# Sums of w_out's quarters made by GpSimd instead of VectorE, in a hybrid decoder layer

## The chip, the cores and the metric

The kernel runs on one core of a Trainium2 chip. What counts is the time of one execution on the device, in microseconds (us). TensorE does the matmuls, VectorE (DVE in the profile), ScalarE (ACT) and GpSimd (POOL) the elementwise work, and SyncE (SP) issues most of the DMAs; SPq is its queue.

## What is computed

One layer over 1024 positions of width 2048. The input is normalised and projected; one half of the projected columns goes through gated DeltaNet attention (group A), the other through a spatial gate in chunks of 128 positions (group B). The two results stand side by side, 2048 wide, and go through the output projection, a residual add and a last norm:

```python
def reference(x, norm_w, w_in, ..., w_out, final_norm_w):
    xn = rms_norm(h, norm_w[l])
    proj = xn @ w_in[l].astype(x.dtype)
    ...
    o_b = u_b * chunked_causal_sgu(v_n, w_spatial[l], b_spatial[l]) * jax.nn.silu(z_b)
    mix = jnp.concatenate([o_a, o_b], axis=-1) @ w_out[l].astype(x.dtype)
    h = h + mix
    return rms_norm(h, final_norm_w)
```

The change touches w_out alone, a 2048 x 2048 matrix in float32.

## The kernel before

The positions are worked in two halves of 512. Each half first does group A, then group B; after both comes one output phase. A matmul in float32 is made of three in a shorter format: each operand is split into a high part (a cast by ScalarE, L136) and a low part (what is left, a subtraction by VectorE, L137), and the three products hi x hi, hi x lo and lo x hi are added in PSUM (L238, L239, L241).

The output projection is done with seven block products instead of eight (Winograd's form of Strassen's scheme). For this the blocks of w_out are needed in four sums, T1 to T4. They are made ahead of time, while group B of each half runs, by the generator `w_sums` (L830): for each of eight k it loads four tiles of 128 x 512, one from each quarter of w_out (L837, tiles `ws{cb}_{k}_{i}`), adds and subtracts in place in a chain of four operations (L839, L840, L842, L843), and stores the four results to a buffer in DRAM, `wc_d` (L846). Half 0 makes the sums of one column block, half 1 those of the other. In the first of the four operations tile 0 takes tile 1 off, in the second tile 1 takes tile 2 off, in the third tile 2 adds tile 0, in the fourth tile 3 takes tile 2 off. So the third needs the first, and the fourth the third.

Tiles 0 and 1 share the buffers with the tag `o`, two of them; tiles 2 and 3 those with the tag `gae`, three. The quarters of the next k can thus be loaded into tiles 0 and 1 only when the stores of this k have landed. Such a round of loads, sums and stores is called a turn here.

At the same time TensorE multiplies the projection's weights. They come in chunks of 128 x 512 (`wr`, loaded at L187 by `w_chunk`), with three buffers for the raw chunk and four for each of its parts `wh` and `wl`. TensorE works twelve matmuls on a chunk. `wr_38_2` is chunk 2 of column tile 38. The list `tasks` holds generators, which `tick` moves on between matmuls; how far they run is told in ticks (`W_SUM0` = 84 ticks before the first turn; then 5, 1, 1 and 3 in a turn). The order on each engine is that of a scheduler, which goes by its own estimates of the durations, within what dependencies allow. Each engine works its list in order, and a DMA that has to wait at the head of SP's queue keeps back all that stand behind it.

Of the kernel before, what the change touches and what calls it, by code (L numbers as in the profile page):

```python
# [12 lines left out]
ALU = mybir.AluOpType  # L13
# [18 lines left out]
def kernel(ctx, tc, x_tok, x_t, w_in, w_v0, w_vb, w_out, conv_w, norm_w, a_log, dt_bias,  # L32
                       hn_w, sgu_w, sgu_b, wsp_t, b_sp, fn_w, out):
    nc = tc.nc
# [739 lines left out]
    def group_b(hf, xs, st):  # L774

        env, sb = {}, {}
        spawn(w_sums([(hf, k) for k in range(HK)]))
        for blk in range(1, 4):
            for k2 in range(KT // 2):
# [46 lines left out]
    def w_quarter(b, cb, k):  # L826

        return w_out[b[1] * 2 + cb, b[0] * HK + k]

    def w_sums(ck):  # L830

        yield W_SUM0
        for cb, k in ck:
            q = {}
            for i, b in enumerate(((1, 1), (0, 1), (0, 0), (1, 0))):
                q[b] = wk.tile([P, 1, T], F32, tag=("o", "gae")[i // 2], bufs=(2, 3)[i // 2], name=f"ws{cb}_{k}_{i}")
                nc.sync.dma_start(q[b], w_quarter(b, cb, k))  # L837
            yield 5
            nc.vector.tensor_tensor(q[1, 1], q[1, 1], q[0, 1], op=ALU.subtract)  # L839
            nc.vector.tensor_tensor(q[0, 1], q[0, 1], q[0, 0], op=ALU.subtract)  # L840
            yield 1
            nc.vector.tensor_tensor(q[0, 0], q[0, 0], q[1, 1], op=ALU.add)  # L842
            nc.vector.tensor_tensor(q[1, 0], q[1, 0], q[0, 0], op=ALU.subtract)  # L843
            yield 1
            for i, b in enumerate(((0, 1), (0, 0), (1, 1), (1, 0))):
                nc.sync.dma_start(wc_d[i, cb, k], q[b].rearrange("p o c -> p (o c)"))  # L846
            yield 3
# [238 lines left out]
```

## Time and profile before

| | us |
|---|---|
| median of 3 runs | 1749.18 (1749.1 to 1756.64) |
| the profiled execution | 1754.24 |
| its span in the trace | 1752.5 |

| engine | busy us | share of the span |
|---|---|---|
| TensorE, matmuls | 1724.6 | 98% |
| VectorE | 1222.7 | 70% |
| ScalarE | 823.5 | 47% |
| GpSimd | 95.3 | 5% |

The busy time is told of the span. Matmuls overlap, so a share of 98% says that TensorE hardly ever stood, not that it went at its peak. TensorE's clock has two levels; the granted clock is told as a share of the upper one. "Idle before" is the time that an engine stood before an instruction, and the name behind the arrow is what released it. The time of a DMA runs from its issue on the queue to its landing.

### The profile page before, as it was taken

The numbers are of one execution on the slowest core, as the hardware profiler recorded it, in microseconds if no ns is written. First come the engines' busy times: TensorE is split into PE (matmuls) and PEld (weight loads), VectorE is DVE, ScalarE is ACT, GpSimd is POOL, SyncE is SP. The second block draws the span as 40 slices with busy tenths as digits, with TensorE's granted clock in tenths as the row PEclk, the third lists the DMA queues.
The fourth block names the chain that finished last, engine by engine and source line by source line (L and its number), as shares of the span: only waits on it lengthen the run. The fifth ranks groups of instructions, "written<-read, shape, count | busy, mean of one in ns | idle before, by whom it ended". The sixth has DMA issues, their size and how long they took to land.

```text
span 1752.5 us, 27530 instructions
## 1 busy us (share of the span) xinstructions
PE 1724.6 (98%) x9334; PEld 1457.0 (83%) x9334; DVE 1222.7 (70%) x3015; ACT 823.5 (47%) x1952; POOL 95.3 (5%) x172
## 2 busy tenths in 40 slices
PE   9999999999999999999999999999999999999997
PEld 8878888888998887887888888899888788888886
DVE  7678697887836654757979789793665544766776
ACT  7573545546434322638555464642432234433454
POOL 1000010010100000000001001010010000000000
PEclk9999999999999999999999999999999999999999
DMA  7454445364533687426553645443268866666565
GB/s 251 107 144 128 115 119 151 97 177 127 133 101 106 198 287 246 131 63 172 138 136 93 169 106 150 136 130 106 67 174 275 263 195 204 214 186 192 160 196 200
DMA packets 190046, 277.99 MB, mean 159 GB/s; under 512 B 38064, under 2 KB 70864, under 8 KB 189648
## 3 DMA queue, kind: packets, MB, share of 16 engines
q1 hardware_dynamic: 185216, 263.60, 51.2%
q0 software_dynamic: 4544, 12.62, 2.9%
q8 instruction: 73, 1.20, 0.3%
q14 instruction: 69, 0.57, 0.1%
q10 hardware_dynamic: 144, 0.01, 0.0%
HBM read 220.54 MB, written 55.61 MB: 158 GB/s over the span
## 4 chain that ended last, share of the span: by engine, by line
PE 78%; DMA 9%; DVE 8%; issue 2%; ACT 2%; SPq 1%; POOL 0%; DVEq 0%; ACTq 0%; POOLq 0%
PE oa L1008 15%; PE acc L238 14%; PE acc L241 14%; PE acc L239 14%; PE vb L794 8%; DMA wr<-w_in 2%; DMA ws<-w_out 2%; DMA wc_d<-ws 2%; PE ds L637 1%; DVE wl L137 1%; PE p L626 1%; DVE cv L416 1%; PE first L307 1%; PE first L306 1%; PE first L308 1%
## 5 line engine op out<-in xcount | busy, mean ns | idle before, releaser
L238 PE MATMUL acc<-xh,wh 128*128 128x512 f32 x1472 | 593.1, 403 | 1.1 <-ACT wh L136 1.1
L241 PE MATMUL acc<-xh,wl 128*128 128x512 f32 x1472 | 579.5, 394 | 11.5 <-DVE wl L137 11.5
L239 PE MATMUL acc<-xl,wh 128*128 128x512 f32 x1472 | 577.2, 392 | 0.0
L136 ACT CAST wh<-wr 128x512 fp32r<-128x512 f32 x368 | 226.5, 617 | 421.2 <-PE acc L239 205.4
L241 PEld LDWEIGHTS acc<-xh,wl 128*128 128x128 f32 x1472 | 278.2, 189 | 73.4 <-DVE wl L137 15.2
L238 PEld LDWEIGHTS acc<-xh,wh 128*128 128x128 f32 x1472 | 278.8, 189 | 58.1 <-issue 3.4
L239 PEld LDWEIGHTS acc<-xl,wh 128*128 128x128 f32 x1472 | 278.6, 189 | 51.8 <-issue 0.2
L137 DVE TENSOR_TENSOR wl<-wr,wh 128x512 fp32r<-128x512 f32 x368 | 250.3, 684 | 96.3 <-ACT wh L136 93.4
L1008 PE MATMUL oa<-who,a 128*128 128x512 f32 x864 | 266.9, 389 | 0.0
L1008 PEld LDWEIGHTS oa<-who,a 128*128 128x128 f32 x864 | 162.3, 188 | 33.6
L1008 PE MATMUL oa<-wlo,a 128*128 128x512 f32 x432 | 168.2, 389 | 0.0
L416 DVE SCALAR_TENSOR_TENSOR cv<-pc,cw,cv 128x511 f32<-128x511 f32 (+1 forms) x144 | 107.1, 744 | 7.5 <-ACT cv L413 5.7
L794 PE MATMUL vb<-whvb,xh 128*128 128x256 f32 x384 | 110.6, 288 | 0.0
L136 ACT CAST who<-wro 128x512 fp32r<-128x512 f32 x108 | 66.7, 618 | 92.7 <-PE oa L1008 71.6
L137 DVE TENSOR_TENSOR wlo<-wro,who 128x512 fp32r<-128x512 f32 x108 | 73.9, 687 | 50.0 <-ACT who L136 49.4
L794 PE MATMUL vb<-whvb,xl 128*128 128x256 f32 x384 | 108.7, 283 | 0.0
L794 PE MATMUL vb<-wlvb,xh 128*128 128x256 f32 x384 | 108.7, 283 | 0.0
L1008 PEld LDWEIGHTS oa<-wlo,a 128*128 128x128 f32 x432 | 81.1, 188 | 16.8
L571 DVE TENSOR_TENSOR fst<-fs 32x31 f32<-32x31 f32 (+15 forms) x248 | 81.0, 327 | 4.4
L573 DVE TENSOR_TENSOR fs<-fs,fst 32x31 f32<-32x31 f32 (+15 forms) x248 | 81.0, 327 | 4.2
L794 PEld LDWEIGHTS vb<-whvb,xh 128*128 128x128 f32 x384 | 73.7, 192 | 0.2
L794 PEld LDWEIGHTS vb<-wlvb,xh 128*128 128x128 f32 x384 | 73.7, 192 | 0.0
(245 smaller groups left out, 2245.5 us busy)
## 6 DMA issues: line engine op xcount, KB each, us to landing
wr<-w_in SPq DMA_DIRECT2D x368, 256.0 KB, 3.4
ws<-w_out SPq DMA_DIRECT2D x64, 256.0 KB, 4.8
wc_d<-ws SPq DMA_DIRECT2D x64, 256.0 KB, 3.3
wro<-wc_d SPq DMA_DIRECT2D x64, 256.0 KB, 2.8
ar<-mix_d SPq DMA_DIRECT2D x56, 256.0 KB, 3.4
wrvb<-w_vb SPq DMA_DIRECT2D x48, 256.0 KB, 2.7
wro<-w_out SPq DMA_DIRECT2D x48, 256.0 KB, 2.7
xr<-x_t SPq DMA_DIRECT2D x32, 256.0 KB, 4.1
```

The lines of the kernel that those rows point to most:

```text
L136: nc.scalar.copy(hi, src)
L137: nc.vector.tensor_tensor(lo, src, hi.bitcast(F32), op=ALU.subtract)
L238: nc.tensor.matmul(acc, hi[:, kk, :], xh, start=(k == 0), stop=False)
L239: nc.tensor.matmul(acc, hi[:, kk, :], xl, start=False, stop=(last and lo is None))
L241: nc.tensor.matmul(acc, lo[:, kk, :], xh, start=False, stop=last)
L306: nc.tensor.matmul(a, xh[:, tsl], vh[:, k2, :], start=first, stop=False)
L307: nc.tensor.matmul(a, xh[:, tsl], vl[:, k2, :], start=False, stop=False)
L416: nc.vector.scalar_tensor_tensor(cv[:, s:], acc[:, :T - s], w, cv[:, s:], op0=ALU.mult, op1=ALU.add)
L571: nc.vector.tensor_tensor(tv, bc(lu[:, k, k + 1:].unsqueeze(2), [32, n, m]), bc(xu[:, k:k + 1, 0:m], [32, n, m]), op=ALU.mult)
L573: nc.vector.tensor_tensor(xu[:, k + 1:, 0:m], xu[:, k + 1:, 0:m], tv, op=ALU.subtract)
L794: nc.tensor.matmul(a, l[:, tsl], r[:, k % 2, :], start=fl, stop=sp_, skip_group_check=True)
L1008: nc.tensor.matmul(acc[t], l[:, tsl], r[:, 0, :], start=fl, stop=sp_, skip_group_check=True)
```

## The change

The four operations of `w_sums` are issued on GpSimd instead of VectorE. Loads, stores, tiles and the numbers of ticks are as before.

```diff
             yield 5
-            nc.vector.tensor_tensor(q[1, 1], q[1, 1], q[0, 1], op=ALU.subtract)
-            nc.vector.tensor_tensor(q[0, 1], q[0, 1], q[0, 0], op=ALU.subtract)
-            yield 1
-            nc.vector.tensor_tensor(q[0, 0], q[0, 0], q[1, 1], op=ALU.add)
-            nc.vector.tensor_tensor(q[1, 0], q[1, 0], q[0, 0], op=ALU.subtract)
+            nc.gpsimd.tensor_tensor(q[1, 1], q[1, 1], q[0, 1], op=ALU.subtract)
+            nc.gpsimd.tensor_tensor(q[0, 1], q[0, 1], q[0, 0], op=ALU.subtract)
+            yield 1
+            nc.gpsimd.tensor_tensor(q[0, 0], q[0, 0], q[1, 1], op=ALU.add)
+            nc.gpsimd.tensor_tensor(q[1, 0], q[1, 0], q[0, 0], op=ALU.subtract)
             yield 1
```

Since the scheduler puts instructions in order by what it thinks of their durations, the order on three engines changes. On VectorE, in the first half, the operations of turn 6 (`ws_6`) stood between the splits of chunks and the work of group B (`s`, `mb`):

```order
 L768 TENSOR_TENSOR mb_4_7091<-s_4_6727,zb_4_7089 128x512
-L839 TENSOR_TENSOR ws_6_0_7211<-ws_6_0_7211,ws_6_1_7213 128x512
 L752 SCALAR_TENSOR_TENSOR s_6_7107<-sp_6_7102,lnw,brow 128x512
-L840 TENSOR_TENSOR ws_6_1_7213<-ws_6_1_7213,ws_6_2_7215 128x512
 L755 TENSOR_TENSOR s_6_7107<-s_6_7107,rb_715 128x512
 L137 TENSOR_TENSOR wl_45_0_7132<-wr_45_0_7129,wh_45_0_7131 128x512
-L842 TENSOR_TENSOR ws_6_2_7215<-ws_6_2_7215,ws_6_0_7211 128x512
-L843 TENSOR_TENSOR ws_6_3_7217<-ws_6_3_7217,ws_6_2_7215 128x512
 L137 TENSOR_TENSOR wl_45_1_7150<-wr_45_1_7147,wh_45_1_7149 128x512
```

All four leave, and the split of chunk 45_0 has none of them ahead of it any more.

On SP's queue, before, the end of the first half's last turn (stores of `ws_7` to `wc_d`, weights `wr`, the next half's input `xr`):

```order
L837 DMA ws_7_3_7339<-w_out 128x512
L187 DMA wr_38_1_7237<-w_in 128x512
L146 DMA xr_2_7600<-x_t 128x512
L846 DMA wc_d<-ws_7_0_7333 128x512
L187 DMA wr_38_2_7255<-w_in 128x512
L846 DMA wc_d<-ws_7_1_7335 128x512
L846 DMA wc_d<-ws_7_2_7337 128x512
L187 DMA wr_38_3_7292<-w_in 128x512
L846 DMA wc_d<-ws_7_3_7339 128x512
```

Weights stand between the stores, wr_38_2 behind the first. The same place on SP's queue after the change:

```order
L837 DMA ws_7_3_7339<-w_out 128x512
L187 DMA wr_38_1_7237<-w_in 128x512
L846 DMA wc_d<-ws_7_0_7333 128x512
L846 DMA wc_d<-ws_7_1_7335 128x512
L846 DMA wc_d<-ws_7_2_7337 128x512
L187 DMA wr_38_2_7255<-w_in 128x512
L846 DMA wc_d<-ws_7_3_7339 128x512
L146 DMA xr_2_7600<-x_t 128x512
L187 DMA wr_38_3_7292<-w_in 128x512
```

Now wr_38_2 stands behind three stores, and wr_38_3 behind all four. The stores of turns 2, 3 and 4 go in the order of tiles 1, 2, 0, 3 in both kernels, those of the other turns in the order 0, 1, 2, 3. On GpSimd's queue the 32 operations of a half stand behind the last DMAs of group A (L436) and ahead of the next half's memsets.

## Rows read from the trace of the kernel before

**Rows 1.** The page's part 1: busy us (share of the span) x instructions.

```profile
PE 1724.6 (98%) x9334; PEld 1457.0 (83%) x9334; DVE 1222.7 (70%) x3015; ACT 823.5 (47%) x1952; POOL 95.3 (5%) x172
```

**Rows 2.** Stretches: us, busy PE, PEld, DVE, ACT, POOL, granted clock, DMA share, GB/s.

```profile
660.00:680.00 20.00, 16.66 (x65) 13.02 (x64) 9.68 (x16) 3.72 (x6) 0.00 (x0) 0.91 0.79 252
...
1380.00:1400.00 20.00, 20.00 (x84) 16.47 (x83) 10.72 (x18) 4.89 (x8) 0.54 (x1) 0.88 0.72 223
```

**Rows 3.** TensorE's timeline: start, us, engine, line, operands [idle before <- releaser].

```profile
667.30 0.50 PE L241 MATMUL acc<-xh,wl 128*128 128x512 f32 x1 [2.84 <-DVE wl L137]
...
677.89 0.50 PE L241 MATMUL acc<-xh,wl 128*128 128x512 f32 x1 [0.51 <-DVE wl L137]
...
1378.63 0.80 PE L241 MATMUL acc<-xh,wl 128*128 128x512 f32 x1 [2.76 <-DVE wl L137]
```

**Rows 4.** ScalarE's timeline: the cast of the chunk of the first stop.

```profile
660.73 0.62 ACT L136 CAST wh<-wr 128x512 fp32r<-128x512 f32 x1 [2.15 <-DMA wr<-w_in]
```

**Rows 5.** VectorE's timeline, first half: sums (ws) and splits (wl).

```profile
599.42 0.69 DVE L839 TENSOR_TENSOR ws<-ws,ws 128x512 f32<-128x512 f32 x1 [2.08 <-DMA ws<-w_out]
...
602.08 0.69 DVE L843 TENSOR_TENSOR ws<-ws,ws 128x512 f32<-128x512 f32 x1
...
664.10 0.69 DVE L839 TENSOR_TENSOR ws<-ws,ws 128x512 f32<-128x512 f32 x1 [4.72 <-DMA ws<-w_out]
...
666.56 0.69 DVE L137 TENSOR_TENSOR wl<-wr,wh 128x512 fp32r<-128x512 f32 x1
...
675.94 0.69 DVE L839 TENSOR_TENSOR ws<-ws,ws 128x512 f32<-128x512 f32 x1 [6.16 <-DMA ws<-w_out]
...
679.68 0.69 DVE L843 TENSOR_TENSOR ws<-ws,ws 128x512 f32<-128x512 f32 x1
...
681.67 0.69 DVE L137 TENSOR_TENSOR wl<-wr,wh 128x512 fp32r<-128x512 f32 x1 [0.70 <-ACT wh L136]
```

**Rows 6.** Waits from 590 to 690: us in total, times, longest.

```profile
DVE ws L839 <- DMA ws<-w_out: 32.5, 8, 6.9
```

**Rows 7.** Waits of SP's queue from 590 to 700: us in total, times, longest.

```profile
SPq L846 <- DVE ws L839: 15.9, 6, 4.3
```

**Rows 8.** GpSimd's groups by shape: busy us, mean ns | idle before.

```profile
L97 POOL TENSOR_SCALAR_AFFINE_SELECT wmt<-wmt 128x1024 f32<-128x1024 f32 x1 | 1.1, 1093 | 12.5 <-DMA wmt<-wsp_t 12.5
...
L70 POOL TENSOR_SCALAR_AFFINE_SELECT tri<-bones 128x128 f32<-128x128 f32 x1 | 0.3, 291 | 0.0
```

**Rows 9.** SP's queue, timeline: three loads in a row; wr_38_2 in either half.

```profile
624.91 1.33 SPq L187 DMA_DIRECT2D wr<-w_in  x3
...
677.86 0.33 SPq L187 DMA_DIRECT2D wr<-w_in  x1
...
1389.33 0.33 SPq L187 DMA_DIRECT2D wr<-w_in  x1
```

**Rows 10.** DMA issues from 600 to 680: count, KB each, median us to landing.

```profile
wc_d<-ws SPq DMA_DIRECT2D x31, 256.0 KB, 3.5
ws<-w_out SPq DMA_DIRECT2D x27, 256.0 KB, 5.3
wr<-w_in SPq DMA_DIRECT2D x25, 256.0 KB, 5.0
```

**Rows 11.** Timelines: TensorE begins chunk 38_2; VectorE, second half, first sum and split 38_2.

```profile
686.63 0.39 PE L238 MATMUL acc<-xh,wh 128*128 128x512 f32 x1
...
1309.13 0.69 DVE L839 TENSOR_TENSOR ws<-ws,ws 128x512 f32<-128x512 f32 x1 [1.14 <-DMA ws<-w_out]
...
1393.16 0.69 DVE L137 TENSOR_TENSOR wl<-wr,wh 128x512 fp32r<-128x512 f32 x1 [0.72 <-ACT wh L136]
...
1398.34 0.39 PE L238 MATMUL acc<-xh,wh 128*128 128x512 f32 x1
```

**Rows 12.** The page's part 6, whole span: weights, median us to landing.

```profile
wr<-w_in SPq DMA_DIRECT2D x368, 256.0 KB, 3.4
```

## The prediction

> **What bounds the kernel now.** The first part of the page says that TensorE is busy in 98% of the span and VectorE in 70% [rows 1]. So VectorE's share says nothing by itself: time is lost only where TensorE waits. The table by stretches and TensorE's timeline show such places in the two stretches in which the sums are made (about 599 to 682 us, and 1309 to 1392 us). In the first TensorE is idle for 2.84 and 0.51 us, in the second for 2.76 us, each time for the low part wl of a weight chunk [rows 3]; after each long stop the granted clock falls from the upper of its two levels (2.4 GHz) to the lower (1.2 GHz) for a while: 0.91 and 0.88 as means of 20 us, which is 1.8 and 2.4 us of work [rows 2]. Together that is 10.3 us, all that a cure of these stretches could give back.
>
> Why was wl late? ScalarE had cast that chunk's high part by 661.35 [rows 4]; VectorE, which makes wl, stood from 659.4 to 664.10 with the first sum (L839) at its head, waiting for a quarter of w_out to land, then did other operations that stand ahead, and made wl only at 666.56 [rows 5]. A wait of the same kind, 6.16 us, ended at 675.94, just before TensorE's second stop. In the first stretch VectorE waited for quarters 32.5 us in all, eight times [rows 6].
>
> The other resource is SP's queue. It holds, in order, weight loads (L187), loads of quarters (L837) and stores of sums (L846). A store at its head waits for its sum, and weights stand behind it: 15.9 us of waiting for L839 alone [rows 7].
>
> **What the change takes away.** 64 operations of 0.69 us leave VectorE, 44 us; that engine was not the bound, so those microseconds count for nothing. What counts is that VectorE no longer waits for quarters with splits behind it. This is worth at most the 10.3 us above.
>
> **What it adds: slower sums ahead of the stores.** The four sums of a turn are a chain. On VectorE the first turn's chain took 3.35 us (599.42 to 602.77), the last one's, with splits between, 4.4 (675.94 to 680.37) [rows 5]. On GpSimd no operation with two inputs is in this trace. Its one-input select took 0.291 us for 128 columns and 1.093 for 1024 [rows 8]: 0.17 fixed and 0.90 ns a column, so 0.63 us for 512. That is the lower bound, if the second input were free: c, the chain, would be 2.5 us. If each input takes its own pass, a sum is 1.09; with a third pass for the result 1.55, c = 6.2. I take two passes and 0.1 for the hand-over to the next sum, 1.2 each, 4.8, and 0.4 more because splits with two inputs run on VectorE beside the chain and one of them (0.69) may hold it up about every second time: **c = 5.2**.
>
> The Trainium skill (GPSIMD Engine Reference, 3.1 Elementwise — side-by-side cycle accounting) has a two-input add of 2048 fp32 columns at 4497 ns; a quarter of that is an estimate of 1.12 us, c = 4.5, by which the sum below would be +5.8 us. No run here shows it yet.
>
> **One turn of the loop.** SP's order after the change [the two fences on SP] has each turn's four stores close together, then the loads of the next quarters, and a quarter's buffer is loaded again only when its store has landed. SP issues free descriptors about 0.45 us apart [rows 9]. In these stretches a store landed in 3.5 us, a quarter in 5.3 and weights in 5.0 [rows 10]. The same bytes over a longer loop load the DMA engines less, so I take 3.3 and 4.6. From one turn's first sum to the next one's:
> - turns 0, 1, 5, 6: c to the last sum, 0.1 to its store, three more issues to the second quarter (1.35), landing 4.6, 0.05: c + 6.1.
> - turns 2, 3, 4, whose first sum is stored third: 0.75c to the third sum, 1.0 until that store goes, 3.3 until it has landed, 0.45 to the second quarter, 4.6: 0.75c + 9.35.
> Seven turns: 4(c + 6.1) + 3(0.75c + 9.35) = 6.25c + 52.45. With VectorE's chain of 3.35 to 4.4 this gives 73.4 to 80.0; measured in the first half were 76.5 (599.42 to 675.94) [rows 5]. So the formula fits the kernel before.
>
> **What TensorE sees.** The last weights in the loop that count are chunk wr_38_2. Before, it stood behind the first store of the last turn; now behind the third, 0.75c + 0.55 after the turn's first sum. It is issued 7c + 53.0 after the first sum of the stretch:
> - first half: 599.42 + 53.0 + 7c against 677.86 [rows 9], later by 7c - 25.4. Its split was ready at 682.36, and TensorE began it at 686.63 [rows 5, 11]: 4.3 us to spare. TensorE is later by 7c - 29.7.
> - second half: 1309.13 + 53.0 + 7c against 1389.33, later by 7c - 27.2; ready at 1393.85, begun at 1398.34, 4.5 to spare [rows 9, 11]: 7c - 31.7.
> Both are measured against TensorE as it went before, with its own stops in it, so nothing has to be taken off for those. Sum: 14c - 61.4, with c = 5.2 it is +11.4 us. After the last stop of each half the clock should stand at the lower level once more, as it did before (1.8 and 2.4 us): +4.2. **Sum +15.6 us.** The profiled execution took 1754.24 us (span 1752.5), which would become about 1769.8; it lay 5.1 over the median, and on the median of 1749.18 the forecast is **1764.8**.
>
> Costs taken as nothing: VectorE's other work moves earlier, under TensorE's matmuls. Behind the sums on GpSimd's queue stand, in the first half, memsets for the next half's tiles, and in the second the four broadcasts of the final norm's weights (L992), which are wanted only when the output phase's second product is finished, a phase later. If that cover were gone, it would cost one landing, some 4.6 us.
>
> **Rivals.** (a) *Both readers hold each other.* If a GpSimd sum and a VectorE operation with two inputs can't read SBUF at once, each chain takes in two splits whole and not the 0.4 of above: c = 4.8 + 2 x 0.69 = 6.2; some 14 x 6.2 - 61.4 + 4.2 = +29.6 us, 1779; with three splits c = 6.9, +39, 1788. For it: three weight loads stand in a row behind some turns' quarters, so their splits fall into the chain. Against it: nothing in this trace shows GpSimd's compute beside VectorE's. The Trainium skill (SBUF — State Buffer, Who interferes with whom) says that a VectorE instruction with two SBUF inputs and a GpSimd instruction that reads SBUF share one port as a lock, the second waiting for the first to end; by that rule it is this rival. The trace of before can't show it.
> (b) *The loop keeps its pace.* c = 4.8 or a little less and quarters that land in 4.0 us: seven turns are 4.2 us shorter in each half, so 14 x 4.8 - 61.4 - 8.4 + 4.2 = +1.6, 1751. For it: over the whole span weights land in 3.4 us [rows 12]. Against it: the bytes of a turn stay, and they nearly fill the DMA engines here.
> (c) *Faster.* The freed VectorE wins, if c is at or under 4.0 (a sum of 1.0 us), because then 14c - 61.4 is under -5 and no stop is left: the 10.3 us come back, 1739. For it: both stops are VectorE's doing. Against it: a sum must then cost less than two passes. That GpSimd doesn't make the sums at all is ruled out by its order.
>
> **How the numbers follow.** A measurement here can tell about 0.5% (8.7 us) from no change. Forecast, c from 4.75 to 5.9 (+9 to +25): 0.5. (a) 0.18. (b), with what lies between 1740 and 1758: 0.21. (c) 0.11. So slower 0.68, same 0.21, faster 0.11. The range 1744 to 1784 leaves out (c) and the upper half of (a), and holds both ends of the landing (0.6 us a turn is 8.4 us).
>
> **What would show it.** After the change: L839 to L843 on GpSimd, at 1.1 to 1.5 us each; the seven turns of a stretch at 82 to 90 us; SP waiting for GpSimd's sums in L846; TensorE stopping several times for 1 to 4 us from about turn 4 on, for high parts wh that wait for weights (L136 waiting for DMA) and no longer for a blocked VectorE. Wrong it would be if the sums are under 1.0 us, if the turns stay at 11 us, or if TensorE has no stops there; if VectorE's splits grow beyond 0.69 us, (a) holds.

## The result and the profile after

The changed kernel took 1769.64 us (median of 4 runs, 1767.08 to 1771.29) against 1750.43 for the kernel before beside it (4 runs, 1749.1 to 1756.64): a ratio of 1.0102, with a 95% interval of 1.0083 to 1.0121. It is slower by 19.2 us. The profiled execution has a span of 1766.5 us. The first part of its page, in the same columns as [rows 1]:

```profile
PE 1728.6 (98%) x9334; PEld 1454.8 (82%) x9334; DVE 1200.1 (68%) x2951; ACT 822.6 (47%) x1952; POOL 186.3 (11%) x236
```

The 64 operations have moved: VectorE has 64 fewer, GpSimd 64 more. TensorE has the same 9334 matmuls. Nothing in this row says why the kernel is slower; the waits do.

**The sums.** The tile's own view of the kernel after (source line, engine, operation, count: shortest / median / longest ns, first and last start):

```profile
L839 POOL TENSOR_TENSOR ws<-ws,ws x16: 1260/1288/1792, 594.7 to 1401.1; 128x512 f32<-128x512 f32 x16
L840 POOL TENSOR_TENSOR ws<-ws,ws x16: 1261/1290/1754, 596.5 to 1402.5; 128x512 f32<-128x512 f32 x16
L842 POOL TENSOR_TENSOR ws<-ws,ws x16: 1265/1298/1838, 597.9 to 1404.3; 128x512 f32<-128x512 f32 x16
L843 POOL TENSOR_TENSOR ws<-ws,ws x16: 1291/1614/1632, 599.6 to 1405.7; 128x512 f32<-128x512 f32 x16
```

A sum takes 1.26 to 1.30 us, or 1.6 to 1.8. The longer ones have company: GpSimd's timeline beside VectorE's in the first and the last turn of the first half (start us, us, engine, line, operands):

```profile
594.67 1.79 POOL L839 TENSOR_TENSOR ws<-ws,ws 128x512 f32<-128x512 f32 x1 [9.95 <-ACT wh L136]
...
599.62 1.29 POOL L843 TENSOR_TENSOR ws<-ws,ws 128x512 f32<-128x512 f32 x1
...
681.43 1.30 POOL L839 TENSOR_TENSOR ws<-ws,ws 128x512 f32<-128x512 f32 x1 [7.93 <-DMA ws<-w_out]
```

```profile
597.35 1.04 DVE L137 TENSOR_TENSOR wl<-wr,wh 128x512 fp32r<-128x512 f32 x1 [2.03 <-ACT wh L136]
...
684.67 1.77 DVE L137 TENSOR_TENSOR wl<-wr,wh 128x512 fp32r<-128x512 f32 x1 [1.28 <-ACT wh L136]
```

A split that begins while a sum runs takes up to 1.8 us (most 1.0 or more) where it took 0.69 [rows 5]; where the split begins first, it is the sum that grows (607.80 and 607.81: a split of 0.69, a sum of 1.84). A chain of four sums lasts 6.24 us in the first turn (594.67 to 600.91) and 5.96 as the mean of the first half's eight; VectorE's lasted 3.15 to 4.5, 3.7 as the mean. From the first turn's first sum to the last turn's, the seven turns of the first half take 86.8 us (76.5 before), those of the second 84.3.

**SP's queue.** Its waits in the whole span, after (us in total, times, longest):

```profile
SPq L846 <- POOL ws L839: 38.1, 10, 5.0
SPq L846 <- POOL ws L840: 31.6, 14, 4.6
SPq L846 <- POOL ws L842: 16.8, 16, 1.6
SPq L846 <- POOL ws L843: 12.0, 16, 1.3
```

and the same four of the kernel before:

```profile
SPq L846 <- DVE ws L839: 33.0, 12, 4.8
...
SPq L846 <- DVE ws L840: 10.9, 16, 2.1
SPq L846 <- DVE ws L842: 4.4, 16, 0.3
SPq L846 <- DVE ws L843: 4.1, 10, 0.8
```

So SP stands 98.5 us with a store at its head whose sum isn't made, against 52.4 before. (With the waits of L837 for a store to land, 6.5 us after and 16.2 before, it is 105.0 against 68.6.) Weights stand behind.

**TensorE's waits**, after, whole span:

```profile
PE acc L238 <- ACT wh L136: 17.7, 10, 5.0
PE acc L241 <- DVE wl L137: 5.5, 7, 2.1
```

Before, these were 1.1 and 11.5 us. The stops for the low part, VectorE's doing, have halved; the new ones are for the high part, which ScalarE can't cast because the weights aren't there. The longest is in turns 1 to 2. TensorE, ScalarE and SP there, three timelines of the kernel after:

```profile
619.08 0.79 PE L238 MATMUL acc<-xh,wh 128*128 128x512 f32 x1 [4.97 <-ACT wh L136]
```

```profile
607.15 0.62 ACT L136 CAST wh<-wr 128x512 fp32r<-128x512 f32 x1 [7.12 <-DMA wr<-w_in]
...
618.41 2.04 ACT L136 CAST wh<-wr 128x512 fp32r<-128x512 f32 x3 [10.11 <-DMA wr<-w_in]
```

```profile
602.79 0.38 SPq L187 DMA_DIRECT2D wr<-w_in  x1
603.22 0.42 SPq L837 DMA_DIRECT2D ws<-w_out  x1
606.38 5.32 SPq L846 DMA_DIRECT2D wc_d<-ws  x4
611.79 0.38 SPq L769 DMA_DIRECT2D mix_d<-mb  x1
612.26 1.40 SPq L837 DMA_DIRECT2D ws<-w_out  x3
613.71 1.38 SPq L187 DMA_DIRECT2D wr<-w_in  x3
```

To be read from the last one upwards: between 602.79 and 613.71 SP issues no weight load, for 10.9 us. SP stands 2.74 us of that ahead of the first store of turn 1, and the four stores take 5.32, each waiting for its sum. The three loads at 613.71 land, ScalarE casts at 618.41, TensorE goes on at 619.08.

**Where the 19 us lie.** Both traces hold the same 9334 matmuls. The start of the same matmul (counted in order of time) in each, us:

| matmul | before | after | after - before | what lies ahead of it |
|---|---|---|---|---|
| 3500 | 607.51 | 602.94 | -4.57 | nothing yet (this execution began earlier) |
| 3650 | 640.50 | 644.04 | +3.53 | first half, stop of turns 1 to 2 |
| 3800 | 679.15 | 681.50 | +2.35 | before has its own stop of 2.84 |
| 3950 | 712.24 | 718.24 | +5.99 | last stops of the first half |
| 4550 | 825.58 | 833.59 | +8.01 | a stop of 2.08 at 828.69 (1.65 before), then the lower clock |
| 7400 | 1299.70 | 1307.28 | +7.58 | nothing, a small gain |
| 7550 | 1332.80 | 1348.40 | +15.61 | second half, stop of turns 1 to 2 |
| 7850 | 1404.69 | 1417.86 | +13.17 | before has its own stop of 2.76 |
| 9200 | 1710.69 | 1724.38 | +13.69 | the end |

From -4.57 to +13.69 it is 18.3 us in these two executions: 10.6 in the first half's sums, 6.1 in the second's, 1.6 between. The same count in the trace of xt_after (below), which differs from the changed kernel in line 143 alone, gives 8.9, 6.5 and -0.9. So a part can differ by a microsecond or two from one execution to the next, and the part between is no effect that both show.

### The profile page after: what moved, and what is told of

Same layout as the page of the kernel before. It is cut to its first block, busy times and chain, and to the rows that moved or that the text cites. A ratio compares the mean times of both kernels' runs of the same rounds, so it can differ in the third digit from the quotient of the medians.

```text
span 1766.5 us, 27536 instructions
## 1 busy us (share of the span) xinstructions
PE 1728.6 (98%) x9334; PEld 1454.8 (82%) x9334; DVE 1200.1 (68%) x2951; ACT 822.6 (47%) x1952; POOL 186.3 (11%) x236
## 5 line engine op out<-in xcount | busy, mean ns | idle before, releaser
L137 DVE TENSOR_TENSOR wl<-wr,wh 128x512 fp32r<-128x512 f32 x368 | 264.5, 722 | 208.1 <-ACT wh L136 206.4
L433 POOL DMA_DIRECT2D swapo<-ut x64 | 47.2, 743 | 271.1 <-DVE ut L428 227.0
```

What stands on the lines that cost most here:

```text
L137: nc.vector.tensor_tensor(lo, src, hi.bitcast(F32), op=ALU.subtract)
L433: eng.dma_start(d.rearrange("r p t (b c) -> b p t r c", c=32)[b], yb.rearrange("p (t r c) -> p t r c", t=NT, c=32))
```

## Experiments

All times are medians beside runs of the kernel before on the same chip (1749.1 to 1750.4 us in every group). "Chain" is the sums of a turn, one after another.

**Two sums more in each turn.** GpSimd adds one quarter back and takes it off again; nothing else changes.

```diff
             nc.gpsimd.tensor_tensor(q[1, 1], q[1, 1], q[0, 1], op=ALU.subtract)
+            nc.gpsimd.tensor_tensor(q[1, 1], q[1, 1], q[0, 1], op=ALU.add)
+            nc.gpsimd.tensor_tensor(q[1, 1], q[1, 1], q[0, 1], op=ALU.subtract)
```

> The changed kernel with two more operations on GpSimd in each chain (tile 1 added back to tile 0 and taken off again, ahead of the first store), so six of 1.29 us instead of four; nothing else. Theory A (the length of the chain holds SP's queue, and weights stand behind it): each of the seven turns and the last one's tail grow by 2.7 us, some 22 us in each half, 44 in all, so about 1810 us, with TensorE idle for wh that waits for weights. Theory B (GpSimd's reading of SBUF slows VectorE's splits, and TensorE waits for those): the splits that a chain meets grow from two to three, some 1 us a turn, 1785 us at most, with TensorE idle for wl.

Measured: 1815.23 us (1811.63 to 1816.23), ratio 1.0368 [1.0344, 1.0392], 45.6 us over the changed kernel. TensorE's and SP's largest waits (whole span):

```profile
PE acc L238 <- ACT wh L136: 41.5, 20, 5.2
```

```profile
SPq L848 <- POOL ws L842: 85.2, 16, 9.5
```

The first sum of the first half's first turn and that of its last turn:

```profile
596.87 1.64 POOL L839 TENSOR_TENSOR ws<-ws,ws 128x512 f32<-128x512 f32 x1 [10.09 <-DMA ws<-w_out]
...
706.05 1.77 POOL L839 TENSOR_TENSOR ws<-ws,ws 128x512 f32<-128x512 f32 x1 [8.42 <-DMA ws<-w_out]
```

The seven turns of the first half take 109.2 us, 22.4 more than in the changed kernel, those of the second 107.6, 23.3 more: together 45.7, which is what the kernel lost. The chain is 9.21 us (mean of the first half's eight), 3.25 more, and 14 x 3.25 = 45.5. So every microsecond of chain is paid in each of the 14 turns, as long as SP's queue stands behind it. The expectation counted the last turn's tail in each half as well, 16 times in all; 16 x 3.25 = 52 is more than was lost. The prediction's formula has 14 times the chain, too, but otherwise made up: 6.25 in seven turns and 0.75 in the last turn's tail.

**The two readers side by side.** A kernel of its own, which computes nothing of the reference: chains of eight operations on 128x512 tiles, alone and at the same time.

> A kernel of its own that computes nothing of the reference: operations of 128x512 float32 on GpSimd (two inputs in SBUF, in place) and on VectorE, in five sections: GpSimd alone, VectorE alone with two inputs in SBUF, both together, VectorE alone with one input in SBUF and one in PSUM, that one together with GpSimd. If the two engines hold each other when both read two tiles in SBUF: alone 1.26 to 1.29 and 0.69 us, together both longer, GpSimd 1.6 or more and VectorE over 1.0, and with the PSUM input as when alone. If they don't: 1.29 and 0.69 in every section.

Measured in one execution, GpSimd's timeline and then VectorE's (one row is a run of back-to-back operations; d<-d,d has both inputs in SBUF, d<-d,pp one in PSUM):

```profile
7.75 10.64 POOL L36 TENSOR_TENSOR g<-g,g 128x512 f32<-128x512 f32 x8 [7.31 <-DVE d L33]
27.57 13.44 POOL L36 TENSOR_TENSOR g<-g,g 128x512 f32<-128x512 f32 x8 [9.19 <-DVE d L33]
55.86 10.69 POOL L36 TENSOR_TENSOR g<-g,g 128x512 f32<-128x512 f32 x8 [14.85 <-DVE d L33]
```

```profile
20.07 5.78 DVE L38 TENSOR_TENSOR d<-d,d 128x512 f32<-128x512 f32 x8
...
27.53 19.12 DVE L38 TENSOR_TENSOR d<-d,d 128x512 f32<-128x512 f32 x16
...
55.82 11.52 DVE L38 TENSOR_TENSOR d<-d,pp 128x512 f32<-128x512 f32 x16
```

Alone, eight sums take 10.64 us on GpSimd (1.33 each) and eight operations 5.78 on VectorE (0.72). Together, GpSimd's eight take 13.44; VectorE is 5.64 us longer at work, enough for 8 of its 16, so it did 8 while GpSimd did 8: one of each in 1.68 us. With one of VectorE's inputs in PSUM neither slows the other (10.69, and 16 in 11.52). So the hold of rival (a) exists, and it is for operations with two SBUF inputs. The Trainium skill (SBUF — State Buffer, Who interferes with whom) says that these two block each other and that one with at most one SBUF input doesn't; the runs agree on both. The Trainium skill (SBUF — State Buffer, SBUF: two separate sides) calls the block one of the whole instruction, which would make a pair 1.33 + 0.72 = 2.05 us; measured it is 1.68, so some of the two overlaps.

**The quarters and the stores on GpSimd's own queue.** The sums stay on GpSimd; its loads (L837) and stores (L846) no longer pass through SP. SP's loads of the second half's x tiles partly go into the gae buffers, where they would now wait on SP's queue for the sums' stores; line 143 keeps those tiles out of gae.

```diff
-                nc.sync.dma_start(q[b], w_quarter(b, cb, k))
+                nc.gpsimd.dma_start(q[b], w_quarter(b, cb, k))
...
-                nc.sync.dma_start(wc_d[i, cb, k], q[b].rearrange("p o c -> p (o c)"))
+                nc.gpsimd.dma_start(wc_d[i, cb, k], q[b].rearrange("p o c -> p (o c)"))
```

> The changed kernel (sums on GpSimd) with the loads of the quarters and the stores of the sums issued on GpSimd's queue instead of SP's, so that SP's queue holds no transfer that waits for a sum; and the second half's x tiles use no buffer of the tag gae, so that none of them waits for the sums. Theory A: TensorE has no stop over 1 us in the two stretches, though a chain takes 6 us or more, and the time is that of the kernel before less its 10 us of stops, 1737 to 1745 us. Theory B: TensorE still waits for wl that GpSimd held up, 1755 to 1770 us.

Measured: 1741.43 us (1740.43 to 1744.46), ratio 0.9951 [0.9932, 0.9970]: faster than the kernel before by 8.4 us, than the changed one by 28.2. One of its stretches (us; busy PE, PEld, DVE, ACT, POOL; granted clock; DMA share; GB/s), then the same and a later one of the changed kernel:

```profile
600.00:620.00 20.00, 20.00 (x94) 16.71 (x93) 11.59 (x13) 4.99 (x8) 15.13 (x21) 1.00 0.74 239
```

```profile
600.00:620.00 20.00, 15.03 (x69) 11.99 (x67) 6.98 (x7) 2.59 (x6) 10.70 (x8) 0.94 0.72 245
...
660.00:680.00 20.00, 17.20 (x72) 12.67 (x70) 6.42 (x9) 3.63 (x6) 6.78 (x5) 1.00 0.84 257
```

TensorE is busy without a break at the upper clock, in both halves' stretches (130.00 of 130 us from 590, 120.00 of 120 from 1300). And yet the turns are slower than in the changed kernel: seven now take 101.2 us (597.0 to 698.2), because the loads wait in line with the sums. The splits are longer too:

```profile
L137 DVE TENSOR_TENSOR wl<-wr,wh 128x512 fp32r<-128x512 f32 x368 | 274.3, 747 | 145.4 <-ACT wh L136 143.5
```

747 ns is the mean of one; it is 722 in the changed kernel and 684 before. Longer splits and longer turns cost TensorE nothing in these stretches, where nothing that it wants soon stands behind them.

Counted by the matmuls of the table above, this kernel gains 5.6 us on the kernel before in the first half's sums (3500 to 3950) and 6.6 in the second's (7400 to 7900). Of this it loses 4.3 again by matmul 8500, at the start of the output phase. There ScalarE waited 5.0 us for the first product's rows (ar<-mix_d landed in 6.5 us, median of 1400 to 1440, against 4.3 before), TensorE stopped once, and the granted clock was 0.91 from 1420 to 1440:

```profile
1425.08 0.50 PE L1008 MATMUL oa<-who,a 128*128 128x512 f32 x1 [2.37 <-DVE pczb L407]
```

No run shows what slowed these rows.

The Trainium skill (SBUF — State Buffer, Summary: rules for kernel authors) speaks against such a queue beside a busy VectorE in its faster modes, since GpSimd writes the descriptors. No row here shows whether VectorE was in those modes. Quarters landed in 5.9 us (median of 595 to 690) against 4.8 in the changed kernel, and stores in 3.0 against 2.4; the kernel was the fastest all the same.

**Is it the queue, or line 143?** Line 143 alone, put into the changed kernel and into the kernel before.

```diff
-        tags = (("cv", 3), ("ut", 2), ("gae", 3), ("kd", 3), ("pc", 4)) + ((), (("bv", 2), ("kc", 2)))[hf == 0]
+        tags = (("cv", 3), ("ut", 2)) + ((), (("gae", 3),))[hf == 0] + (("kd", 3), ("pc", 4)) + ((), (("bv", 2), ("kc", 2)))[hf == 0]
```

> The changed kernel with one other edit alone, the one that gp_own_queue also holds: the second half's x tiles no longer use the gae buffers. Theory A (the queue that issues the quarters and stores made the difference of gp_own_queue): no change against the changed kernel, 1767 to 1773 us, with the two stops of about 5 us for wh at turns 1 to 2 of each half still there. Theory B (the tags of the x tiles gave the gain): 1750 us or less.

> The kernel before with the tags of the second half's x tiles changed as in ve_own_queue, and nothing else. Theory A (ve_own_queue lost by its queue): 1747 to 1754 us, as before. Theory B (the tags cost it the time): 1770 us or more.

Measured: 1767.72 us (ratio 1.0110 [1.0088, 1.0132]) and 1750.13 us (1.0003 [0.9989, 1.0016]). Neither moves. Line 143 by itself is worth nothing, and what gp_own_queue gained is the queue's.

**The same queue with the sums on VectorE.** This tells whether the queue alone is the cure.

> The kernel before (sums on VectorE) with the same move of loads and stores to GpSimd's queue and the same buffers for x. Theory A: SP's queue is free, but VectorE still stands with a sum at its head until quarters have landed, and splits stand behind it: stops for wl as in the kernel before, 1745 to 1760 us. Theory B gives about the same. If the stops of the kernel before came from SP's queue alone, they are gone: 1740 us.

Measured: 1785.57 us (1783.06 to 1787.88), ratio 1.0198 [1.0171, 1.0225]. The expectation missed. VectorE's wait from 590 to 700, and TensorE's in the whole span:

```profile
DVE ws L839 <- DMA ws<-w_out: 44.4, 8, 6.9
```

```profile
PE acc L241 <- DVE wl L137: 37.0, 15, 5.1
```

SP is free here, but VectorE has a sum at its head that waits for a quarter (44.4 us; 32.5 before [rows 6]), and the splits stand behind it. The cure of SP's queue is lost again on VectorE's.

**Half of the sums on each engine.** L839 and L840 on GpSimd, L842 and L843 on VectorE.

> Two of the four sums of each turn (L839, L840) on GpSimd, two (L842, L843) on VectorE. Theory A (the length of the chain ahead of SP's stores decides): a chain of 2 x 1.4 + 2 x 0.75 = 4.3 us between VectorE's 3.35 to 4.4 and GpSimd's 5.96, and chunk wr_35_3 back between the stores of turn 0; so between the two kernels, 1750 to 1762 us, stops of 5 us at turns 1 to 2 gone or under 3 us. Theory B (any sum on GpSimd costs by holding VectorE's splits, whatever the chain): half of the 64 sums, half of the loss or more plus VectorE's own waiting, 1762 us or more, with stops that wait for wl.

Measured: 1767.17 us (1766.29 to 1768.93), ratio 1.0105 [1.0090, 1.0120]: no better than all four on GpSimd. The size that my theory gave was wrong, and the rival's number came, but not for the rival's reason: the splits keep 687 ns, so nothing holds them up while they run. VectorE's timeline shows what does, and TensorE's wait in the whole span what it costs (11.5 before):

```profile
645.17 0.69 DVE L842 TENSOR_TENSOR ws<-ws,ws 128x512 f32<-128x512 f32 x1 [6.51 <-POOL ws L840]
...
646.50 1.29 DVE L137 TENSOR_TENSOR wl<-wr,wh 128x512 fp32r<-128x512 f32 x2
```

```profile
PE acc L241 <- DVE wl L137: 18.9, 11, 4.5
```

For 6.51 us it stands with a sum that waits for GpSimd, and TensorE stops for 2.12 us, until 647.24, for the split behind it. The chain is shorter and the turns are (79.7 us for seven in the first half), and the stop of turns 1 to 2 is gone, as the theory of SP's queue has it; the loss comes back through VectorE's head.

**Only the stores, or only the loads, on GpSimd's queue.**

> The changed kernel with only the stores (L846) issued on GpSimd's own queue; the loads of quarters (L837) stay on SP's queue. SP no longer waits for a sum, but a load still waits at its head until the store that frees its buffer has landed, with weights behind it. Theory A (any wait for the turn's chain at SP's head holds the weights, the sum's or the landing's): it keeps some of the loss, 1752 to 1772 us, with SP waiting in L837. Theory B (only the stores' wait for sums counts): as gp_own_queue, 1737 to 1746 us.

> gp_own_queue with the stores (L846) back on SP's queue; only the loads of the quarters (L837) are on GpSimd's queue. Theory A (what counts is whether SP's head waits for a turn's chain): SP waits in L846 for GpSimd's sums again, for longer than in the changed kernel, since the turns are longer (13 to 15 us), so 1770 us or more. Theory B (taking SP's 64 loads of quarters off its queue is what gained): 1750 us or less.

(The second of them has line 143 as well.) Measured: 1778.44 us (ratio 1.0168 [1.0150, 1.0186]) with only the stores moved, 1801.53 us (1.0297 [1.0274, 1.0321]) with only the loads moved. SP's largest wait at sums or quarters in each, whole span, stores first:

```profile
SPq L837 <- DMA wc_d<-ws: 112.1, 51, 5.8
```

```profile
SPq L846 <- POOL ws L839: 90.3, 14, 8.1
```

Without the stores SP waits no longer for sums, but its loads of quarters wait for the stores that free their buffers: 112.1 us, where the changed kernel waits 98.5 for sums. The time lies 6 us above the upper end that I had given. Without the loads it waits for the sums of turns that have become longer. As long as either half of the turn is in SP's queue, that queue waits for the whole turn.

**Two sums more, with everything on GpSimd's queue.** The dose of the first experiment, where nothing stands behind it.

> gp_own_queue with two more sums in each turn (add the second quarter back to the first, take it off again), as six_sums did to the changed kernel, where they cost 45.6 us. Here loads and stores of the sums stand on GpSimd's own queue. Theory A (a sum's time costs only through what waits behind it in SP's queue): the turns grow from 14.5 to about 17 us and the time stays within 1738 to 1750 us, the upper part if the second half's sums come late for the output phase. Theory B (GpSimd's sums cost through VectorE's splits or the port, at some 0.7 us a sum added): 1760 us or more.

Measured: 1766.35 us (1765.15 to 1767.55), ratio 1.0100 [1.0081, 1.0119]. Neither theory's number. But nearly all of the loss is in two places:

```profile
PE oa L1010 <- DVE pczb L407: 18.0, 1, 18.0
```

```profile
1440.01 1.09 POOL L848 DMA_DIRECT2D wc_d<-ws  x2
```

```profile
1442.40 1.14 ACT L136 CAST a<-ar 128x512 fp32r<-128x512 f32 x2 [19.85 <-DMA wc_d<-ws]
```

In the two stretches of sums TensorE is busy throughout (130.00 of 130 us from 590 to 720, 120.00 of 120 from 1300 to 1420). Only at the ends of the halves it stops, for 3.5 and 18.0 us. The last stores go at 1440.01, while the output phase began at 1427; its first product puts activations into the same o and gae buffers that hold the sums, and ScalarE waited 19.85 us there for the stores. (TensorE's wait is put down to pczb, the operation of VectorE that ended last; VectorE had itself waited 12.35 us for ScalarE's cast.) In gp_own_queue the last stores go at 1407.61, 32.4 us earlier, and ScalarE has no wait for them. So theory A holds within the stretches, for the 45.6 us of the first experiment are gone there, and the upper end that I gave it missed the price of the date: the loop has to be done before the output phase takes its buffers.

## Why the prediction was right, point by point

- **Direction and cause: right, and shown.** VectorE's waits were cured (TensorE's stops for wl 11.5 to 5.5 us), and longer chains ahead of SP's stores took more than that back. Adding to the chain adds 14 times as much; taking the turn out of SP's queue gives back all of it and the cure besides, 8.4 us under the kernel before. The cure was sized too small: 10.3 us were allowed for it, and gp_own_queue gained 12.2 in the two stretches, before it lost 4.3 in the output phase. The prediction left out a stop of 0.42 us at 1352.87, and its second stretch [rows 2] begins at 1380, 1.4 us behind the end of the stop. An earlier stretch of the kernel before has more of the low clock:

```profile
1370.00:1390.00 20.00, 17.24 (x64) 13.73 (x64) 8.62 (x15) 3.73 (x6) 0.48 (x1) 0.83 0.80 261
```

- **The total: +15.6 us forecast, +18.3 in the profiled pair, +19.2 of the medians.** Within the range. By parts, forecast with the clock: 8.5 in the first half (10.6 measured), 7.1 in the second (6.1), nothing between (1.6). Most of the 1.6 is the clock: behind the stop of 2.08 us at 828.69 it fell (0.91 from 820 to 840), and behind the 1.65 of the kernel before it did not (1.00). In xt_after the stop there is 1.47 us, the clock stays at 1.00, and nothing is lost between.
- **The chain, c: mis-sized.** Forecast 5.2 us, measured 5.96, just above the 4.75 to 5.9 to which the forecast's chance belonged. Most of the error is the sum itself: it takes 1.29 us undisturbed and 1.37 from one to the next, where 1.2 was taken with the hand-over, so four are 5.4 us and not 4.8. The hold-ups, set at 0.4, are the other 0.6. The estimate from the Trainium skill (GPSIMD Engine Reference, 3.1 Elementwise — side-by-side cycle accounting), 1.12 for a sum, was lower still. Rival (a)'s hold is real, and by the prediction's own sign, splits beyond 0.69 us, it holds: each chain of the first half has one or two sums that grow by 0.3 to 0.6 us. Its c, 6.2, was the nearer one, 0.24 too long, though a held pair isn't fully one after the other. Its time, 1779, was not: 9 us too long, where the forecast of 1764.8 was 5 too short.
- **The turns: mis-sized the other way.** Stores were taken at 3.3 us and landed in 2.6, quarters at 4.6 and landed in 4.8 (medians of 600 to 680). With c = 5.96 the prediction's formula gives 6.25 x 5.96 + 52.45 = 89.7 us for seven turns; they took 86.8. Most of the 2.9 us, 2.4, lies in turns 2, 3 and 4, which took 13.0 us each where the formula has 13.8; the landings by themselves explain 0.7 of the 2.9, and the rest stays open. The forecast of 85.0 was near because its errors cancel in part, which is luck. With c right and the rest of the formula as it was, the forecast would have been +26 us.
- **The place: half wrong.** wr_38_2's issue by SP and TensorE's start on its chunk, in the timelines of after:

```profile
686.33 0.39 SPq L187 DMA_DIRECT2D wr<-w_in  x1
```

```profile
690.66 0.50 PE L238 MATMUL acc<-xh,wh 128*128 128x512 f32 x1 [1.50 <-ACT wh L136]
```

  With the 4.57 us by which this execution is ahead, 690.66 is 8.6 us later than in [rows 11], where 6.7 was forecast. But the long stops were to come from turn 4 on, and they came in turns 1 to 2, in both halves. SP's order at turn 1 of the first half had shown why (- before, + after; ws_1 are the quarters of turn 1, wr weights):

```order
 L837 DMA ws_1_1_6624<-w_out 128x512
 L837 DMA ws_1_3_6628<-w_out 128x512
+L187 DMA wr_35_3_6730<-w_in 128x512
 L837 DMA ws_2_2_6753<-w_out 128x512
-L187 DMA wr_43_0_6757<-w_in 128x512
-L187 DMA wr_43_1_6775<-w_in 128x512
 L846 DMA wc_d<-ws_1_0_6622 128x512
 L846 DMA wc_d<-ws_1_1_6624 128x512
-L187 DMA wr_43_2_6793<-w_in 128x512
 L846 DMA wc_d<-ws_1_2_6626 128x512
 L846 DMA wc_d<-ws_1_3_6628 128x512
```

  wr_35_3, which had stood between turn 0's stores, and wr_43_0 to wr_43_2 were all moved behind a turn's four stores. The prediction read only the place of the last chunk. That spoils the place and not the sum: what TensorE loses early it doesn't lose again while it waits for a queue that runs late anyway. This last point is argued from the table of matmuls; no run has the early stop alone.
- **The clock: wrong in place.** 1.8 and 2.4 us were forecast after the last stop of each half. The clock fell instead after the long stops of turns 1 to 2 (4.97 and 4.8 us idle) and stayed up after the last ones (2.3 us and less). The stretches of the changed kernel at the first half's long stop and at the second half's, in the columns as above:

```profile
620.00:640.00 20.00, 19.64 (x83) 15.99 (x83) 11.28 (x14) 4.80 (x8) 7.14 (x6) 0.89 0.79 256
...
1330.00:1350.00 20.00, 15.18 (x54) 11.78 (x53) 9.39 (x10) 4.25 (x7) 8.49 (x7) 0.83 0.75 252
```

  0.83 over 20 us is 3.4 us at the upper clock; 0.94 (the stretch from 600, shown beside gp_own_queue's) and 0.89 are together the same 3.4. A part of that fell into the stop itself. By TensorE's timeline matmuls start 0.43 us apart behind these stops and 0.23 later, and the work lost so is 2.6 and 3.0 us (in the kernel before 1.7 and 2.9). As this falls early in a half, it is part of the lateness at its end and not to be added to it.
- **Splits: wrong.** They were to stay at 0.69 us unless rival (a) held; they grew to as much as 1.8 where they began beside a running sum. That growth by itself costs nothing: in gp_own_queue the splits are longer still (747 ns against 722) and TensorE doesn't stop.

What happened in one table; the waits are those at the head of a queue that also carries weights or splits:

| kernel | sums on | SP waits for the turn | VectorE waits for the turn | us |
|---|---|---|---|---|
| gp_own_queue | GpSimd | no | no | 1741.4 |
| before | VectorE | for sums, 52.4 | for quarters, 32.5 in half 1 | 1750 |
| half_sums | both | for sums, 70.5 | for quarters and sums, 35.6 in half 1 | 1767.2 |
| after | GpSimd | for sums, 98.5 | no | 1769.6 |
| stores_gp | GpSimd | for stores to land, 112.1 | no | 1778.4 |
| ve_own_queue | VectorE | no | for quarters, 44.4 in half 1 | 1785.6 |
| loads_gp | GpSimd | for sums, 147.3 | no | 1801.5 |

## What to carry to other kernels

When an operation is moved to a slower engine, don't ask whether that engine has room; ask whose queue waits for the result, and what stands behind it there: each microsecond of this chain was paid 14 times through SP's queue and not at all once its loads, sums and stores stood in a queue of their own. A side job moves as a whole, with its DMAs, or it leaves its wait in the queue it came from. Once it is off, look for its date: with two sums more it held the output phase up for 18 us.

## What the runs showed of the hardware

A 128x512 fp32 sum with two SBUF inputs takes 1.28 us on GpSimd (1.33 from one to the next) and 0.69 on VectorE. Run side by side they go one for one, a pair in 1.68 us; with one of VectorE's inputs in PSUM each keeps its own pace. GpSimd issues a load or a store of 256 KB in 0.54 to 0.56 us of its own time. TensorE's clock went to its lower level after stops of 4.97 and 4.82 us in the changed kernel, where matmuls then start 0.43 us apart and not 0.23 (2.6 and 3.0 us of work lost), and after stops of 2.84 and 2.76 in the kernel before [rows 3] (1.7 and 2.9). Shorter stops of the changed kernel differ: behind 2.29 us at 679.52 the granted clock stayed at 1.00 (660 to 700), behind 2.08 at 828.69 it was 0.91 (820 to 840).
